# A decoder layer on one core: queries, keys and the MLP's first product computed with tokens on the output's partitions and transposed on TensorE

## The chip, the core and the metric

The kernel runs on one core of one Trainium2 chip. A core has five engines with their own queues: TensorE (PE in the profile; its loads of stationary operands are shown apart as PEld), VectorE (DVE), ScalarE (ACT), GpSimd (POOL) and SyncE (SP), which issues most transfers. The metric is the device time of one execution in microseconds (us). The figure given for a kernel is the median of its runs.

## The reference

One decoder layer for 256 tokens of width 2048. Two mixers with 8 heads each of 128 columns share a normalised input. With 256 tokens and blocks of 256 keys the first mixer is causal attention with ALiBi. The second is causal attention with a cumulated forget gate.

```python
hn = rms_norm(x, norm_mix_g)
z = hn @ w_in
q_a, k_a, v_a, q_b, k_b, v_b, f_logit, g_a, g_b = jnp.split(z, split_idx, axis=-1)
a = moba_attention(split_heads(q_a), split_heads(k_a), split_heads(v_a))
bfx = forgetting_attention(split_heads(q_b), split_heads(k_b), split_heads(v_b), f_logit, b_forget)
merged = jax.nn.sigmoid(g_a) * (merge_heads(a) @ w_proj_a) + jax.nn.sigmoid(g_b) * (merge_heads(bfx) @ w_proj_b)
x = x + merged @ w_out
hm = rms_norm(x, norm_mlp_g)
x = x + jnp.square(jax.nn.relu(hm @ w_up)) @ w_down
return rms_norm(x, norm_final_g)
```

All inputs are float32. `w_in` has 2048 x 10248 elements (four blocks of 1024 columns in it are queries and keys), `w_up` 2048 x 8192, `w_down` 8192 x 2048.

## The kernel before

Every weight is read once, as one stream. `load` brings a chunk of 1 MB (`raw`, 4 buffers) on SP's queue. `emit_split` makes of each half of a chunk a high part `whi` (ACT, line 89) and a low part `wlo` (DVE, line 90), which TensorE takes as float32r; there are 4 buffers of each. The activations are kept in high and low parts too, and a product is the sum of three: high by high, high by low, low by high.

`plan` lists the blocks of the stream in the order of use: values, forget gate and first gate columns, then queries and keys, the other gates, the projections `pa` and `pb`, `w_out`, and the MLP in five groups (`FF_GROUPS`: 16, 16, 16, 8 and 8 tiles of 128 hidden columns), where the `up` blocks of a group stand ahead of its four `down` blocks. A block is worked off half a chunk at a time. After each half `boundary` counts one step, emits the split of a later half, and then emits what tasks are due (`at(step, function)`): attention, head by head in four tasks, transposes of activations, and the like. So the order of the matmuls and of all that stands between them is written out in the program, and each engine runs its queue in that order.

There are two forms of a block:

- `tok_block` (matmul at line 230): the activations of 128 tokens are stationary, 512 columns of weights stream past. The output has tokens on its partitions. One tile of 128 rows of the weights by 512 columns takes 6 matmuls of 512 columns (two halves of the tokens, three products). A half chunk has 2 such tiles, so 12 matmuls.
- `col_block` (lines 243 and 246): 128 columns of weights are stationary, the activations of all 256 tokens stream past, high and low side by side (512 columns, line 243), and then the high ones alone for the low weights (256 columns, line 246). The output has the columns on its partitions, which is what attention and the `down` blocks want as their stationary operands. 128 rows by 512 columns of weights take 4 such pairs. ACT and DVE then add the two halves of the sum (`qk_evac`, `up_evac`).

Queries, keys and `up` are of the second form, everything else of the first. `x_rows` spreads the tokens' scale over the partitions for `qk_evac`. Transposes on TensorE are used for x (line 260), the probabilities (line 412), the merged output (line 483) and x after attention (line 260 again). A result that is read as an operand of `pa`, `pb` or `down` is written to a tile of the pool `head` (tile name `hd`).

Of the kernel before, what the change touches and what calls it, by code (L numbers as in the profile page):

```python
# [7 lines left out]
FT = mybir.dt.float32  # L8
FR = mybir.dt.float32r
AF = mybir.ActivationFunctionType  # L10
OP = mybir.AluOpType
# [4 lines left out]
NT = 2  # L16
# [23 lines left out]
def hybrid_layer(ctx: ExitStack, tc, x, norm_mix_g, w_in, b_forget, w_proj_a, w_proj_b, w_out,  # L40
# [4 lines left out]
    head = ctx.enter_context(tc.tile_pool(name="head", bufs=17))  # L45
# [51 lines left out]
    def seq_tok(src, c0, ncol, nk, k0=0):  # L97
        first = len(halves)
        for k in range(k0, k0 + nk, 4):
            add_chunk(src, k, 4, c0, ncol)  # L100
        return first, len(halves)

    def seq_col(src, c0):
        first = len(halves)
        for k in range(0, KT, 8):
            add_chunk(src, k, 8, c0, 256)
        return first, len(halves)
# [6 lines left out]
    # The 8 forget columns share two blocks of 260 with the first 512 gate columns.  # L114
    plan.append(("fg", 0, seq_tok(w_in, C_F, FG, KT)))
    plan.append(("g", (FG - NH, FG), seq_tok(w_in, C_F + FG, FG, KT)))
    for m in range(2):
        for n in range(NH // 2):
            plan.append(("q", m * NH + 2 * n, seq_col(w_in, (C_QA, C_QB)[m] + n * 256)))
            plan.append(("k", m * NH + 2 * n, seq_col(w_in, (C_KA, C_KB)[m] + n * 256)))  # L120
# [8 lines left out]
    for gi, g in enumerate(FF_GROUPS):  # L129
        for f in range(0, g, 2):  # L130
            plan.append(("up", f0 + f, seq_col(w_up, (f0 + f) * 128)))
        for n in range(4):
            plan.append(("down", (gi, f0, g, n), seq_tok(w_down, n * 512, 512, g, f0)))
        f0 += g
    assert f0 * 128 == DFF

# [65 lines left out]
    def at(n, f, *a):  # L202
        tasks.append((n, f, a))
# [13 lines left out]
    # Tokens on partitions: the activations are stationary, the weights stream.  # L217
# [16 lines left out]
    # Columns on partitions: the weights are stationary, hi and lo activations stream side by side.  # L234
    def col_block(rng, act, ps):
        n = rng[1] - rng[0]
        kh = halves[rng[0]][2]
        for i in range(*rng):
            hi, lo = split[i]
            for kk in range(kh):  # L240
                k = (i - rng[0]) * kh + kk
                for c in range(2):
                    nc.tensor.matmul(ps[c], hi[:, kk, c * 128:(c + 1) * 128],  # L243
                                     act[:, k].rearrange("p s t -> p (s t)"),
                                     start=k == 0, stop=False)
                    nc.tensor.matmul(ps[c][:, S:], lo[:, kk, c * 128:(c + 1) * 128], act[:, k, 0, :],  # L246
                                     start=False, stop=k == n * kh - 1)
            boundary()

# [5 lines left out]
    def transpose_scaled(src, k0, dst, gbase, stepwise=False):  # L255
        """Two column tiles of src (tokens on partitions), transposed, times g, as hi and lo."""
        p = psum.tile([128, 2, S], FT, name="aux")
        for kk in range(2):
            for tok in range(NT):
                nc.tensor.transpose(p[:, kk, tok * 128:(tok + 1) * 128],  # L260
                                    src[:, tok, (k0 + kk) * 128:(k0 + kk + 1) * 128], ident)
        gs = [gcol[:, gbase + k0 + kk:gbase + k0 + kk + 1] for kk in range(2)]

        def high(kk):
            nc.scalar.activation(dst[:, k0 + kk, 0, :], p[:, kk, :], AF.Copy, scale=gs[kk])

# [26 lines left out]
    rk = const.tile([128, S], FT, name="rk")  # L293
    rq = const.tile([128, S], FT, name="rq")
# [15 lines left out]

    def x_rows():
        p = psum.tile([128, 512], FT, name="aux")
        for tok in range(NT):
            nc.tensor.transpose(p[:, tok * 128:(tok + 1) * 128],
                                rstd[:, tok:tok + 1].to_broadcast([128, 128]), ident)
        nc.scalar.activation(rk, p[:, :S], AF.Copy)
        nc.scalar.activation(rq, p[:, :S], AF.Copy, scale=SCALE)
# [4 lines left out]
    at(15, x_rows)  # L322

# [10 lines left out]
    def forget(ps):  # L334
        z = const.tile([128, NT, NH], FT, name="fz")
        e = const.tile([128, NT, NH], FT, name="fe")
        u = const.tile([128, NT, NH], FT, name="fu")
        l = const.tile([128, NT, NH], FT, name="fl")
        for tok in range(NT):
            nc.vector.scalar_tensor_tensor(z[:, tok], ps[tok][:, :NH], rstd[:, tok:tok + 1], bB[:, tok],  # L340
                                           op0=OP.mult, op1=OP.add)
        # log_sigmoid(z) = min(z, 0) - log1p(exp(-|z|)), log1p(e) = log(u) + (e - (u - 1)) / u
        nc.vector.scalar_tensor_tensor(e, z, -1.0, z, op0=OP.mult, op1=OP.min)
        nc.scalar.activation(e, e, AF.Exp)
        nc.vector.tensor_scalar(u, e, 1.0, None, op0=OP.add)
# [25 lines left out]
    def fox_bias(h):  # L371
        p = psum.tile([128, 512], FT, name="aux")
        nc.tensor.matmul(p[:, :S], sel[:, h:h + 1].to_broadcast([64, 128]), cumT, start=True, stop=True)  # L373
        nb = work.tile([128, 384], FT, name="nb")
# [4 lines left out]
    # Scores: columns 0:128 are rows 0:128 on keys 0:128, columns 128:384 rows 128:256 on all keys.  # L379
# [28 lines left out]
    def att_transpose(h):  # L408
# [4 lines left out]
        pt = work.tile([128, 384], FT, name="probT")  # L413
# [3 lines left out]
    def att_values(h):  # L417
# [5 lines left out]
        o = head.tile([128, 2, S], FR, name="hd")  # L423
        nc.scalar.activation(o[:, 0], p[:, :S], AF.Copy)
        nc.vector.tensor_tensor(o[:, 1], p[:, :S], o[:, 0].bitcast(FT), OP.subtract)
        heads[h] = o
# [8 lines left out]

    def qk_evac(kind, h0, ps):
        for c in range(2):
            if kind == "q":
                qk = head.tile([128, 2, S], FT, name="hd")
                heads[h0 + c] = qk  # L440
            qk = heads[h0 + c]
            t = work.tile([128, S], FT, name="ta")
            nc.scalar.activation(t, ps[c][:, :S], AF.Copy)
            nc.vector.tensor_tensor(t, t, ps[c][:, S:], OP.add)
            dst = qk[:, 0 if kind == "q" else 1]
            nc.vector.tensor_tensor(dst, t, rq if kind == "q" else rk, OP.mult)
            state[kind, h0 + c] = dst

# [55 lines left out]
    def up_evac(f, ps):  # L504
        for c in range(2):
            t = work.tile([128, S], FT, name="ta")
            nc.scalar.activation(t, ps[c][:, :S], AF.Copy)  # L507
            nc.vector.tensor_tensor(t, t, ps[c][:, S:], OP.add)  # L508
            u = work.tile([128, S], FT, name="tu")
            nc.vector.scalar_tensor_tensor(u, t, 0.0, t, op0=OP.max, op1=OP.mult)  # L510
            h = head.tile([128, 2, S], FR, name="hd")
            nc.scalar.activation(h[:, 0], u, AF.Copy)  # L512
            nc.vector.tensor_tensor(h[:, 1], u, h[:, 0].bitcast(FT), OP.subtract)  # L513
            hT[f + c] = h
# [14 lines left out]
    def final_add(tok, i):  # L529
        """fst[:, tok, 0] collects the mean square; the first three blocks and EPS come at once."""  # L530
# [22 lines left out]
    for kind, n, rng in plan:  # L553
# [19 lines left out]
        elif kind in ("q", "k"):  # L573
            ps = mm_banks()
            col_block(rng, xT, ps)
            qk_evac(kind, n, ps)
            if kind == "k":
                attention(now[0] + 2, n)
                attention(now[0] + 6, n + 1)
# [7 lines left out]
        elif kind in ("pa", "pb"):  # L587
            m = kind == "pb"
            ps = mm_banks()
            tok_block(rng, lambda k, s, tok: heads[m * NH + k][:, s, tok * 128:(tok + 1) * 128], ps)  # L590
# [16 lines left out]
        elif kind == "up":  # L607
            ps = mm_banks()
            col_block(rng, x1T, ps)
# [7 lines left out]
        else:  # L617
# [4 lines left out]
            def act_h(k, s, tok):  # L622
                return hT[f0 + k][:, s, tok * 128:(tok + 1) * 128]
# [57 lines left out]
```

## Time and profile before

| | |
|---|---|
| time, median of 3 runs | 1386.27 us (1386.09 to 1386.78) |
| span of the profiled execution, first to last instruction | 1385.9 us |
| TensorE busy with matmuls | 1374.7 us, 99% |
| loads of stationary operands (PEld), 6955 of them | 1167.0 us, 84% |
| VectorE busy | 809.8 us, 58% |
| ScalarE busy | 636.6 us, 46% |
| read from HBM | 256.99 MB, 187 GB/s over the span |

The profiled execution's own time is its span, 1385.9 us, and 0.4 us less than the median of the runs. A busy share counts a matmul from its start to a modelled end, and ends overlap the next start. How much of the span a matmul takes is read from the start of one to the start of the next, which is what the chain of work in order of time adds up: each of its pieces has a start, a length and the instructions in it.

### The profile page before, as it was taken

How to read it: one execution, taken by the hardware profiler on the slowest of the kernel's cores; microseconds unless marked ns; L12 is line 12 of the kernel's file. 1: busy time of each engine (PE TensorE's matmuls, PEld its weight loads, DVE VectorE, ACT ScalarE, POOL GpSimd, SP SyncE). 2: the span in 40 equal slices, each digit the busy share in tenths (PEclk: the TensorE clock that was granted, in tenths of full speed). 3: DMA queues.
4: the chain of work that ended last, by engine and by line, in shares of the span. 5: the costliest groups of instructions: out<-in, count | busy, mean ns of one | idle time of the engine just before them, and what ended most of it. 6: DMA issues, size and time to landing. Idle time of an engine off the chain costs nothing.

```text
span 1385.9 us, 17183 instructions
## 1 busy us (share of the span) xinstructions
PE 1374.7 (99%) x6955; PEld 1167.0 (84%) x6955; DVE 809.8 (58%) x1057; ACT 636.6 (46%) x853; POOL 5.8 (0%) x22
## 2 busy tenths in 40 slices
PE   9999999999999999999999999999999999999997
PEld 7889888888888888888888888888888888888886
DVE  6546666666444456655666555665556655566576
ACT  5545544544544443445445434444344443344442
POOL 0000000000000000000000000000000000000000
PEclk9999999999999999999999999999999999999999
DMA  8638555454556565555665655655555565655552
GB/s 307 209 109 258 180 155 175 151 161 153 181 187 199 192 243 194 179 201 180 211 189 183 209 186 182 190 197 191 187 178 183 185 210 195 200 183 186 179 184 90
DMA packets 182223, 260.20 MB, mean 188 GB/s; under 512 B 4576, under 2 KB 109312, under 8 KB 181760
## 3 DMA queue, kind: packets, MB, share of 16 engines
q1 hardware_dynamic: 181424, 255.94, 56.6%
q10 hardware_dynamic: 720, 3.16, 0.6%
q8 instruction: 54, 0.88, 0.3%
q14 instruction: 25, 0.20, 0.0%
HBM read 256.99 MB, written 2.10 MB: 187 GB/s over the span
## 4 chain that ended last, share of the span: by engine, by line
PE 99%; DMA 0%; issue 0%; DVE 0%; SPq 0%; POOLq 0%; POOL 0%; ACT 0%; ACTq 0%
PE mm L230 57%; PE mm L243 26%; PE mm L246 13%; PE aux L384 1%; PE aux L421 0%; PE aux L260 0%; DMA rows<-in_x_dram 0%; PE aux L412 0%; PE aux L422 0%; PE aux L383 0%; PE aux L483 0%; PE aux L373 0%; POOLq L676 0%; POOL fst L540 0%; DVE rows L522 0%
## 5 line engine op out<-in xcount | busy, mean ns | idle before, releaser
L90 DVE TENSOR_TENSOR wlo<-raw,whi 128x1024 fp32r<-128x1024 f32 (+2 forms) x489 | 586.2, 1205 | 470.0 <-ACT whi L89 468.0
L89 ACT ACTIVATE whi<-raw 128x1024 fp32r<-128x1024 f32 (+2 forms) x489 | 505.8, 1042 | 473.0 <-PE mm L230 374.9
L243 PE MATMUL mm<-big,whi 128*128 128x512 f32 x1536 | 547.7, 400 | 0.0
L246 PE MATMUL mm<-big,wlo 128*128 128x256 f32 x1536 | 431.1, 281 | 0.0
L230 PE MATMUL mm<-whi,hd 128*128 128x512 f32 x1280 | 394.4, 388 | 0.0
L243 PEld LDWEIGHTS mm<-big,whi 128*128 128x128 f32 x1536 | 288.4, 188 | 69.0
L230 PE MATMUL mm<-whi,big 128*128 128x512 f32 (+1 forms) x1088 | 326.4, 380 | 0.0
L246 PEld LDWEIGHTS mm<-big,wlo 128*128 128x128 f32 x1536 | 290.2, 189 | 0.6
L230 PEld LDWEIGHTS mm<-whi,hd 128*128 128x128 f32 x1280 | 239.9, 188 | 49.5
L230 PE MATMUL mm<-wlo,hd 128*128 128x512 f32 (+1 forms) x640 | 248.2, 388 | 0.0
L230 PEld LDWEIGHTS mm<-whi,big 128*128 128x128 f32 x1088 | 200.8, 188 | 37.7
L230 PE MATMUL mm<-wlo,big 128*128 128x512 f32 (+1 forms) x544 | 205.5, 378 | 0.0
L230 PEld LDWEIGHTS mm<-wlo,hd 128*128 128x128 f32 x640 | 120.2, 188 | 24.4
L230 PEld LDWEIGHTS mm<-wlo,big 128*128 128x128 f32 x544 | 102.5, 188 | 18.3
L512 ACT ACTIVATE hd<-tu 128x256 fp32r<-128x256 f32 x64 | 26.7, 418 | 62.6 <-DVE tu L510 62.6
L507 ACT ACTIVATE ta<-mm 128x256 f32<-128x256 f32 x64 | 24.1, 376 | 47.3 <-PE mm L246 47.3
L513 DVE TENSOR_TENSOR hd<-tu,hd 128x256 fp32r<-128x256 f32 x64 | 27.2, 425 | 31.0 <-ACT hd L512 31.0
L508 DVE TENSOR_TENSOR ta<-ta,mm 128x256 f32<-128x256 f32 x64 | 26.8, 418 | 20.4 <-ACT ta L507 20.4
L398 ACT ACTIVATE prob<-prob,stat 128x128 f32<-128x128 f32 (+1 forms) x32 | 14.3, 448 | 48.7 <-DVE stat L396 48.7
L510 DVE SCALAR_TENSOR_TENSOR tu<-ta 128x256 f32<-128x256 f32 x64 | 27.2, 425 | 2.2
L518 DVE SCALAR_TENSOR_TENSOR rows<-mm,inv,rows 128x512 f32<-128x512 f32 x32 | 22.5, 744 | 0.0
L414 ACT ACTIVATE probT<-aux 128x384 f32<-128x384 f32 x16 | 7.9, 492 | 30.9 <-PE aux L412 30.9
(117 smaller groups left out, 341.2 us busy)
## 6 DMA issues: line engine op xcount, KB each, us to landing
raw<-in_w_in_dram SPq DMA_DIRECT2D x72, 1024.0 KB, 5.1
raw<-in_w_up_dram SPq DMA_DIRECT2D x64, 1024.0 KB, 5.6
raw<-in_w_down_dram SPq DMA_DIRECT2D x64, 1024.0 KB, 5.2
raw<-in_w_out_dram SPq DMA_DIRECT2D x16, 1024.0 KB, 5.1
raw<-in_w_proj_a_dram SPq DMA_DIRECT2D x8, 1024.0 KB, 5.1
raw<-in_w_proj_b_dram SPq DMA_DIRECT2D x8, 1024.0 KB, 5.0
raw<-in_w_in_dram SPq DMA_DIRECT2D x8, 520.0 KB, 3.8
raw<-in_w_in_dram SPq DMA_DIRECT2D x7, 512.0 KB, 8.0
```

Source lines behind the costliest of these rows:

```text
L89: nc.scalar.activation(hi[:, j:j + n], r[:, j:j + n], AF.Copy)
L90: nc.vector.tensor_tensor(lo[:, j:j + n], r[:, j:j + n], hi[:, j:j + n].bitcast(FT), OP.subtract)
L230: nc.tensor.matmul(p[:, :nc_], a, w[:, kk, c0:c0 + nc_], start=first and j == 0, stop=last and j == 2)
L243: nc.tensor.matmul(ps[c], hi[:, kk, c * 128:(c + 1) * 128], act[:, k].rearrange("p s t -> p (s t)"), start=k == 0, stop=False)
L246: nc.tensor.matmul(ps[c][:, S:], lo[:, kk, c * 128:(c + 1) * 128], act[:, k, 0, :], start=False, stop=k == n * kh - 1)
L398: nc.scalar.activation(t[:, sl], t[:, sl], AF.Exp, bias=st[:, tok:tok + 1], accum_out=st[:, 2 + tok:3 + tok])
L507: nc.scalar.activation(t, ps[c][:, :S], AF.Copy)
L508: nc.vector.tensor_tensor(t, t, ps[c][:, S:], OP.add)
L510: nc.vector.scalar_tensor_tensor(u, t, 0.0, t, op0=OP.max, op1=OP.mult)
L512: nc.scalar.activation(h[:, 0], u, AF.Copy)
L513: nc.vector.tensor_tensor(h[:, 1], u, h[:, 0].bitcast(FT), OP.subtract)
L518: nc.vector.scalar_tensor_tensor(t, ps[tok], inv2[:, tok:tok + 1], t, op0=OP.mult, op1=OP.add)
```

## The change

Queries, keys and `up` use `tok_block` too. Their weights are loaded in blocks of 512 columns. The products then have tokens on the partitions: ACT moves them out of PSUM (scaled by the token's own factor, or through relu and square), and two steps later eight 128 x 128 transposes on TensorE (`transposed_pair`, twice) turn four tiles of columns. For `up` ACT and DVE then make the high and low parts. `col_block` and `x_rows` are gone. The pool of 17 tiles becomes one of 9 tiles of two column tiles each (tile name `pr`). A key block now serves four heads, whose tasks start four steps after it and stand four steps apart, as they did before. Comments are taken out, so that line numbers move: the matmul of `tok_block` is line 230 before and 224 after, the new transposes are line 411, the evacuation of `up` lines 493, 494, 501 and 502.

```diff
-    head = ctx.enter_context(tc.tile_pool(name="head", bufs=17))
+    pair = ctx.enter_context(tc.tile_pool(name="pair", bufs=9))
...
-        for n in range(NH // 2):
-            plan.append(("q", m * NH + 2 * n, seq_col(w_in, (C_QA, C_QB)[m] + n * 256)))
-            plan.append(("k", m * NH + 2 * n, seq_col(w_in, (C_KA, C_KB)[m] + n * 256)))
+        for n in range(NH // 4):
+            plan.append(("q", m * NH + 4 * n, seq_tok(w_in, (C_QA, C_QB)[m] + n * 512, 512, KT)))
+            plan.append(("k", m * NH + 4 * n, seq_tok(w_in, (C_KA, C_KB)[m] + n * 512, 512, KT)))
...
-        for f in range(0, g, 2):
-            plan.append(("up", f0 + f, seq_col(w_up, (f0 + f) * 128)))
+        for f in range(0, g, 4):
+            plan.append(("up", f0 + f, seq_tok(w_up, (f0 + f) * 128, 512, KT)))
...
-    # Columns on partitions: the weights are stationary, hi and lo activations stream side by side.
-    def col_block(rng, act, ps):
...
-                for c in range(2):
-                    nc.tensor.matmul(ps[c], hi[:, kk, c * 128:(c + 1) * 128],
-                                     act[:, k].rearrange("p s t -> p (s t)"),
-                                     start=k == 0, stop=False)
-                    nc.tensor.matmul(ps[c][:, S:], lo[:, kk, c * 128:(c + 1) * 128], act[:, k, 0, :],
-                                     start=False, stop=k == n * kh - 1)
...
+        nc.vector.tensor_scalar(rstq, rstd, SCALE, None, op0=OP.mult)
-
-    def x_rows():
-        p = psum.tile([128, 512], FT, name="aux")
-        for tok in range(NT):
-            nc.tensor.transpose(p[:, tok * 128:(tok + 1) * 128],
-                                rstd[:, tok:tok + 1].to_broadcast([128, 128]), ident)
...
+    def transposed_pair(src, i):
+        p = psum.tile([128, 2, S], FT, name="aux")
+        for c in range(2):
+            for tok in range(NT):
+                nc.tensor.transpose(p[:, c, tok * 128:(tok + 1) * 128],
+                                    src[:, tok, (i + c) * 128:(i + c + 1) * 128], ident)
+        return p
+
     def qk_evac(kind, h0, ps):
+        t = work.tile([128, NT, 512], FT, name="ta")
+        for tok in range(NT):
+            r = rstq if kind == "q" else rstd
+            nc.scalar.activation(t[:, tok], ps[tok], AF.Copy, scale=r[:, tok:tok + 1])
+        for i in range(0, 4, 2):
+            at(now[0] + 2, qk_transpose, kind, h0 + i, t, i)
+
+    def qk_transpose(kind, h, t, i):
+        p = transposed_pair(t, i)
...
+        nc.scalar.activation(qk[:, :, m], p, AF.Copy)
...
     def up_evac(f, ps):
-        for c in range(2):
-            t = work.tile([128, S], FT, name="ta")
-            nc.scalar.activation(t, ps[c][:, :S], AF.Copy)
-            nc.vector.tensor_tensor(t, t, ps[c][:, S:], OP.add)
-            u = work.tile([128, S], FT, name="tu")
-            nc.vector.scalar_tensor_tensor(u, t, 0.0, t, op0=OP.max, op1=OP.mult)
-            h = head.tile([128, 2, S], FR, name="hd")
-            nc.scalar.activation(h[:, 0], u, AF.Copy)
-            nc.vector.tensor_tensor(h[:, 1], u, h[:, 0].bitcast(FT), OP.subtract)
-            hT[f + c] = h
+        t = work.tile([128, NT, 512], FT, name="ta")
+        for tok in range(NT):
+            nc.scalar.activation(t[:, tok], ps[tok], AF.Relu)
+        nc.scalar.activation(t, t, AF.Square)
+        for i in range(0, 4, 2):
+            at(now[0] + 2, up_transpose, f, t, i)
+
+    def up_transpose(f, t, i):
+        p = transposed_pair(t, i)
+        h = pair.tile([128, 2, 2, S], FR, name="pr")
+        nc.scalar.activation(h[:, :, 0], p, AF.Copy)
+        nc.vector.tensor_tensor(h[:, :, 1], p, h[:, :, 0].bitcast(FT), OP.subtract)
+        hT[(f + i) // 2] = h
...
-            col_block(rng, xT, ps)
+            tok_block(rng, act_x, ps)
             qk_evac(kind, n, ps)
             if kind == "k":
-                attention(now[0] + 2, n)
-                attention(now[0] + 6, n + 1)
+                for i in range(4):
+                    attention(now[0] + 4 + 4 * i, n + i)
...
-            col_block(rng, x1T, ps)
+            tok_block(rng, lambda k, s, tok: hl(x1T, k, s, tok), ps)
             up_evac(n, ps)
```

TensorE inside the `up` blocks of the last group, before (`big` is x after attention, transposed; each pair is one `col_block` step):

```order
L243 MATMUL mm<-big,whi 128x512
L246 MATMUL mm<-big,wlo 128x256
L243 MATMUL mm<-big,whi 128x512
L246 MATMUL mm<-big,wlo 128x256
L243 MATMUL mm<-big,whi 128x512
L246 MATMUL mm<-big,wlo 128x256
```

and after (`ta` is the evacuated product of the block before, tokens on partitions):

```order
L224 MATMUL mm<-wlo,big 128x512
L224 MATMUL mm<-whi,big 128x512 x2
L224 MATMUL mm<-wlo,big 128x512
L224 MATMUL mm<-whi,big 128x512
L411 MATMUL aux<-ident,ta 128x128 x8
L224 MATMUL mm<-whi,big 128x512
L224 MATMUL mm<-wlo,big 128x512
L224 MATMUL mm<-whi,big 128x512 x2
```

All matmuls are 512 columns wide now, and once in a block of 96 of them eight transposes stand in between.

TensorE where the first `down` block of the last group begins, before (`hd` is the squared relu, transposed):

```order
L243 MATMUL mm<-big,whi 128x512
L246 MATMUL mm<-big,wlo 128x256
L230 MATMUL mm<-whi,hd 128x512
L230 MATMUL mm<-wlo,hd 128x512
L230 MATMUL mm<-whi,hd 128x512 x2
```

and after, two half chunks into that block, with the numbers of the tiles (`pr_9617` is what is made of the first four transposes, `aux_9612`):

```order
L224 MATMUL mm_9577<-wlo_9551,pr_9467 128x512
L224 MATMUL mm_9577<-whi_9550,pr_9467 128x512
L411 MATMUL aux_9612<-ident_122,ta_9572 128x128 x4
L411 MATMUL aux_9620<-ident_122,ta_9572 128x128 x4
L224 MATMUL mm_9576<-whi_9568,pr_9617 128x512
L224 MATMUL mm_9576<-wlo_9569,pr_9617 128x512
L224 MATMUL mm_9576<-whi_9568,pr_9617 128x512
```

In the two groups of 8 tiles the transposes of the last `up` block stand directly ahead of the matmuls that read their result; in the groups of 16 tiles four half chunks lie between.

ACT over one `up` block, before (two column tiles):

```order
L507 ACTIVATE ta<-mm 128x256
L512 ACTIVATE hd<-tu 128x256
L507 ACTIVATE ta<-mm 128x256
L512 ACTIVATE hd<-tu 128x256
L89 ACTIVATE whi<-raw 128x1024 x4
```

and after (four column tiles):

```order
L493 ACTIVATE ta<-mm 128x512 x2
L494 ACTIVATE ta<-ta 128x1024
L89 ACTIVATE whi<-raw 128x1024 x2
L501 ACTIVATE pr<-aux 128x2x256 x2
L89 ACTIVATE whi<-raw 128x1024 x6
```

The evacuation comes in two parts with two splits of weights between them, where the transposes are waited for.

## Rows read from the trace of the kernel before

**Rows 1.** The page: busy time of TensorE, its granted clock, the chain by engine.
```profile
PE 1374.7 (99%) x6955; PEld 1167.0 (84%) x6955; DVE 809.8 (58%) x1057; ACT 636.6 (46%) x853; POOL 5.8 (0%) x22
...
PEclk9999999999999999999999999999999999999999
...
PE 99%; DMA 0%; issue 0%; DVE 0%; SPq 0%; POOLq 0%; POOL 0%; ACT 0%; ACTq 0%
```

**Rows 2.** Groups by shape on TensorE: names, shapes, count, busy us, mean ns, idle.
```profile
L243 PE MATMUL mm<-big,whi 128*128 128x512 f32 x1536 | 547.7, 400 | 0.0
L246 PE MATMUL mm<-big,wlo 128*128 128x256 f32 x1536 | 431.1, 281 | 0.0
L230 PE MATMUL mm<-whi,hd 128*128 128x512 f32 x1264 | 391.6, 389 | 0.0
...
L230 PEld LDWEIGHTS mm<-whi,hd 128*128 128x128 f32 x1280 | 239.9, 188 | 49.5
```

**Rows 3.** Chain in order of time (start us, length us, what), MLP and output projection.
```profile
514.67 0.87 PE aux L483 x8
...
537.36 0.87 PE aux L483 x8
...
648.94 19.09 PE mm L230 x84
...
757.69 87.08 PE mm L230 x384
935.22 87.06 PE mm L230 x384
1112.72 87.06 PE mm L230 x384
1245.00 43.58 PE mm L230 x192
1333.79 33.73 PE mm L230 x150
```

**Rows 4.** The same chain from the query and key blocks to attention's end.
```profile
119.99 4.28 PE mm L230 x36
...
329.47 2.79 PE mm L230 x12
...
339.89 2.77 PE mm L230 x12
...
353.05 5.50 PE mm L230 x24
358.88 5.47 PE mm L230 x24
365.01 149.66 PE mm L230 x660
```

**Rows 5.** Timeline around one run of eight transposes (start us, busy us, what).
```profile
514.51 1.04 PE L483 MATMUL aux<-ident,big 128*128 128x128 f32 x8
515.14 1.09 ACT L486 ACTIVATE big<-aux 128x512 fp32r<-128x512 f32 x2 [2.10 <-PE aux L483]
515.30 0.47 PE L230 MATMUL mm<-whi,hd 128*128 128x512 f32 x1
515.77 1.29 DVE L487 TENSOR_TENSOR big<-aux,big 128x512 fp32r<-128x512 f32 x2 [1.48 <-ACT big L486]
```

**Rows 6.** Groups by shape on ACT: split of weights, evacuation of 512 columns.
```profile
L89 ACT ACTIVATE whi<-raw 128x1024 fp32r<-128x1024 f32 x471 | 494.7, 1057 | 459.9 <-PE mm L230 362.8 <-PE mm L243 95.0 <-DMA raw<-in_w_in_dram 1.1
L464 ACT ACTIVATE big<-mm,rstd 128x512 f32<-128x512 f32 x14 | 9.5, 688 | 5.7 <-PE mm L230 5.7
```

**Rows 7.** Stretches: busy us of PE, PEld, DVE, ACT, POOL; granted clock; DMA share; GB/s.
```profile
8.50:12.50 4.00, 4.00 (x15) 3.13 (x13) 3.42 (x7) 2.70 (x5) 0.00 (x0) 0.63 1.07 376
514.00:538.00 24.00, 24.00 (x116) 19.99 (x115) 15.08 (x17) 9.64 (x11) 0.00 (x0) 1.00 0.55 188
```

**Rows 8.** Chain in order of time: the first twelve matmuls, and twelve later ones.
```profile
8.73 4.37 PE mm L230 x12
13.53 2.77 PE mm L230 x12
```

More of the change, by code (lines that the diff above doesn't have):

```diff
@@ L101, in seq_tok @@
         return first, len(halves)
[L103 to L107, printed above, removed]
     plan = []
@@ L232, in tok_block @@
             boundary()
-    def col_block(rng, act, ps):
[L236 to L241, printed above, removed]
-                for c in range(2):
-                    nc.tensor.matmul(ps[c], hi[:, kk, c * 128:(c + 1) * 128],
-                                     act[:, k].rearrange("p s t -> p (s t)"),
-                                     start=k == 0, stop=False)
-                    nc.tensor.matmul(ps[c][:, S:], lo[:, kk, c * 128:(c + 1) * 128], act[:, k, 0, :],
-                                     start=False, stop=k == n * kh - 1)
-            boundary()
     def mm_banks():
@@ L292, in hybrid_layer @@
     rstd = const.tile([128, NT], FT, name="rstd")
-    rk = const.tile([128, S], FT, name="rk")
-    rq = const.tile([128, S], FT, name="rq")
+    rstq = const.tile([128, NT], FT, name="rstq")
     def mean_square(acc, dst):
@@ L309, in x_rstd @@
         nc.gpsimd.tensor_tensor(rstd, mean, expo, op=OP.pow)
-    def x_rows():
-        p = psum.tile([128, 512], FT, name="aux")
-        for tok in range(NT):
-            nc.tensor.transpose(p[:, tok * 128:(tok + 1) * 128],
-                                rstd[:, tok:tok + 1].to_broadcast([128, 128]), ident)
-        nc.scalar.activation(rk, p[:, :S], AF.Copy)
-        nc.scalar.activation(rq, p[:, :S], AF.Copy, scale=SCALE)
+        nc.vector.tensor_scalar(rstq, rstd, SCALE, None, op0=OP.mult)
     for j in range(4):
@@ L321, in hybrid_layer @@
     at(11, x_rstd)
-    at(15, x_rows)
     state = {}
@@ L373, in fox_bias @@
         nc.tensor.matmul(p[:, :S], sel[:, h:h + 1].to_broadcast([64, 128]), cumT, start=True, stop=True)
-        nb = work.tile([128, 384], FT, name="nb")
+        nb = work.tile([128, 384], FT, name="nb", bufs=1)
         nc.vector.scalar_tensor_tensor(nb[:, :128], p[:, :128], -1.0, mask[:, :128], op0=OP.mult, op1=OP.add)
@@ L412, in att_transpose @@
             nc.tensor.transpose(p[:, i * 128:(i + 1) * 128], t[:, i * 128:(i + 1) * 128], ident)
-        pt = work.tile([128, 384], FT, name="probT")
+        pt = work.tile([128, 384], FT, name="probT", bufs=1)
         nc.scalar.activation(pt, p[:, :384], AF.Copy)
@@ L422, in att_values @@
         nc.tensor.matmul(p[:, 128:S], v[:, 1, sl], pt[:, S:], start=False, stop=True)
-        o = head.tile([128, 2, S], FR, name="hd")
+        if h % 2 == 0:
+            heads[h // 2] = pair.tile([128, 2, 2, S], FR, name="pr")
+        o = heads[h // 2][:, h % 2]
         nc.scalar.activation(o[:, 0], p[:, :S], AF.Copy)
         nc.vector.tensor_tensor(o[:, 1], p[:, :S], o[:, 0].bitcast(FT), OP.subtract)
-        heads[h] = o
     def attention(n0, h):
@@ L434, in attention @@
         at(n0 + 5, att_values, h)
-    def qk_evac(kind, h0, ps):
-        for c in range(2):
[L438 to L441, printed above, removed]
-            t = work.tile([128, S], FT, name="ta")
-            nc.scalar.activation(t, ps[c][:, :S], AF.Copy)
-            nc.vector.tensor_tensor(t, t, ps[c][:, S:], OP.add)
-            dst = qk[:, 0 if kind == "q" else 1]
-            nc.vector.tensor_tensor(dst, t, rq if kind == "q" else rk, OP.mult)
-            state[kind, h0 + c] = dst
+    def transposed_pair(src, i):
[5 more added lines that the diff above has]
+        return p
+    def qk_evac(kind, h0, ps):
+        t = work.tile([128, NT, 512], FT, name="ta")
[6 more added lines that the diff above has]
+        p = transposed_pair(t, i)
+        if kind == "q":
+            state["qk", h] = pair.tile([128, 2, 2, S], FT, name="pr")
+        qk = state["qk", h]
+        m = 0 if kind == "q" else 1
+        nc.scalar.activation(qk[:, :, m], p, AF.Copy)
+        for c in range(2):
+            state[kind, h + c] = qk[:, c, m]
+        if kind == "k":
+            del state["qk", h]
     gz = merged = x1 = x1T = fin = None
@@ L504, in up_evac @@
     def up_evac(f, ps):
-        for c in range(2):
-            t = work.tile([128, S], FT, name="ta")
-            nc.scalar.activation(t, ps[c][:, :S], AF.Copy)
-            nc.vector.tensor_tensor(t, t, ps[c][:, S:], OP.add)
-            u = work.tile([128, S], FT, name="tu")
-            nc.vector.scalar_tensor_tensor(u, t, 0.0, t, op0=OP.max, op1=OP.mult)
-            h = head.tile([128, 2, S], FR, name="hd")
-            nc.scalar.activation(h[:, 0], u, AF.Copy)
-            nc.vector.tensor_tensor(h[:, 1], u, h[:, 0].bitcast(FT), OP.subtract)
-            hT[f + c] = h
+        t = work.tile([128, NT, 512], FT, name="ta")
[10 more added lines that the diff above has]
+        hT[(f + i) // 2] = h
     def down_evac(n, ps, tok):
@@ L589, in hybrid_layer @@
             ps = mm_banks()
-            tok_block(rng, lambda k, s, tok: heads[m * NH + k][:, s, tok * 128:(tok + 1) * 128], ps)
+            tok_block(rng, lambda k, s, tok: hl(heads[(m * NH + k) // 2], k % 2, s, tok), ps)
             if merged is None:
@@ L622, in act_h @@
             def act_h(k, s, tok):
-                return hT[f0 + k][:, s, tok * 128:(tok + 1) * 128]
+                return hl(hT[(f0 + k) // 2], k % 2, s, tok)
             if not last:
```

## The prediction

> **What bounds the kernel now.** I read the page first. TensorE is busy 99% of the span, the chain that ended last lies on it for 99%, and the clock granted to it is full in all 40 slices [rows 1]. No other engine is near: DVE 58%, ACT 46%. So the time is the sum of TensorE's queue, instruction after instruction, and the question is what each costs there. The mean durations do not say it: a 512-wide matmul of the column form "takes" 400 ns and its 256-wide partner 281 ns, a 512-wide one of the token form 389 ns [rows 2], but 1536 pairs at 681 ns would be 1046 us, three quarters of the span, for work that the chain holds for about 540. These ends are modelled and overlap. I therefore read the chain in order of time, where a piece runs from the start of its first instruction to the start of the next piece [rows 3, 4]. The reader is to see there that nothing waits: the pieces follow each other without holes through the MLP.
>
> **The price of a matmul, token form.** A group of four `down` blocks is 384 matmuls and 87.06 us [rows 3], so 226.7 ns each. The 192 of a small group take 43.58 us [rows 3], 227.0 ns.
>
> **The price of the column form.** Between two `down` groups lie the `up` blocks. From 757.69 + 87.08 to 935.22 are 90.45 us; from 935.22 + 87.06 to 1112.72 are 90.44; from 1112.72 + 87.06 to 1245.00 are 45.22; from 1245.00 + 43.58 to 1333.79 are 45.21; and from 648.94 + 19.09 to 757.69 are 89.66, with one run of eight transposes of x in it [rows 3]. Together 360.98 us. A large group has 256 pairs, so 353 ns a pair. Per 128 columns of weights both forms stream 768 columns; the column form does it in 2 matmuls (353 ns), the token form in 1.5 (340 ns). The change wins 13 ns per pair.
>
> **The price of the transposes.** Two runs of eight (line 483) start at 514.67 and 537.36, 22.69 us apart, with the 96 matmuls of one block between them [rows 3]. 96 at 226.7 ns are 21.76, so a run costs 0.93 us, including the slower matmuls just behind it. The chain gives 0.87 for the run alone [rows 3]. I take 0.93; the new runs are the same instruction, size and place, between two token-form matmuls. The change adds 24 runs: 16 behind the `up` blocks, 8 behind the query and key blocks.
>
> **MLP.** After: 1536 matmuls, four times 87.06 or 348.2 us, and 17 runs (16 new, the one of x), 15.8 us: 364.0. Before: 361.0. Plus 3.0 us.
>
> **Queries, keys and attention.** From 119.99 + 4.28 to 365.01 are 240.74 us [rows 4]. In them lie 512 pairs, 132 matmuls of the gates (the nine chain pieces from 329.47 to 358.88, counts added [rows 4]), and all tasks of 16 heads. After, the pairs are 768 matmuls; with the 132 they are 900, or 204.0 us. The tasks of the heads are the same instructions, now all between token-form matmuls; their price there is to be read at the end of the stretch. From 339.89 to 353.05 are 13.16 us with 48 matmuls (10.88) and one full set of a FoX head's tasks: 2.28 us. From 353.05 to 358.88 are 24 matmuls and one transpose of probabilities, 0.39; from 358.88 to 365.01 24 matmuls and one product with the values, 0.69 [rows 4]. A MoBA head has scores (priced as the values), transpose and values: 1.77. Eight of each are 32.4 us. With 8 runs of transposes (7.4) the sum is 243.8. Plus 3.1 us. `x_rows` goes with two transposes, a quarter of a run: minus 0.2.
>
> **A new wait.** The queue order shows that in the two groups of 8 tiles the last transposes stand directly ahead of the matmuls that read what ACT and DVE make of them. The nearest rows are those of line 483, the same shapes [rows 5]: from the run's start, ACT begins its first copy at 0.63 us and needs half of 1.09, so the high part is there at 1.2; DVE begins at 1.26 and needs half of 1.29, so the low part is there at 1.9. TensorE would go on at 0.79. It waits until 1.2 and then loads the operand, 188 ns [rows 2]: about 0.6 us; the third matmul wants the low part at 1.85 and gets it at 1.9 plus the load, about 0.3 more. 0.9 us in each of two places, 1.8 in all. Bounds: nothing, if the copy is earlier than in those rows, and 2 us a place, if one split of 1.06 us [rows 6] happens to stand ahead of the copy. A gain is excluded, since nothing waits there now. In the three groups of 16 four half chunks (10.9 us) lie between, which covers the 1.9.
>
> **Costed at nothing.** The evacuations: behind each block ACT has two moves of 0.69 us, a square of 1.06 (priced as a split of the same size [rows 6]) and perhaps a split of 1.06, 3.5 us, and the transposes come two half chunks, 5.4 us, behind the block's end. If that cover went, TensorE would wait in 24 places. DVE loses three operations for each column tile and gains one wide one for two; it was not on the path. The weights' loads keep their bytes; of ACT's idle time ahead of the splits the data accounts for 1.1 us in all [rows 6].
>
> **Sum.** 3.0 + 3.1 - 0.2 + 1.8 = 7.7 us on the profiled 1385.9, which lies 0.4 us under the median; so 1386.3 + 7.7, and the predicted time is 1394.0 us, 0.55% slower. The two effects nearly cancel: 2304 matmuls in place of 1536 pairs win about 18 us, 24 runs of transposes cost 22, the waits and the dearer neighbourhood of the heads' tasks are the rest.
>
> **Rivals.** (1) *A shorter interval of the token form in its new place; not slower.* For it: the column form has two speeds in the same program, 88.8 us for the first `up` group (89.66 less 0.87) and 90.45 for the second [rows 3], so an interval is not fixed by shape alone. Against it: every long token stretch shown lies at 226.7 to 227.0 ns [rows 3], with different activations. 2.1 ns less on each of 2304 matmuls (4.9 us) would bring the time within 0.2% of before, 3.3 ns to 1386; below 222 ns the change would be faster by more than that. 0.10: 0.06 for no difference, about 1387, 0.04 for faster, about 1383.
>
> (2) *The clock falls at the transposes.* At the start of the program TensorE ran at a granted share of 0.63 on average, that is partly at 1.2 GHz and partly at 2.4, after it had stood idle for data [rows 7]; there 12 matmuls took 4.37 us where later 2.77 [rows 8], 1.6 us more. If each of the 24 runs did the same, 38 us: 1432. The trace speaks against it: with line 483's runs in the stretch the clock is 1.00 [rows 7]. The Trainium skill ("TensorE: Matmul & The Clock Gate", Part 4: PE-mode transpose) says that a transpose takes some 275 ns in a kernel and does not count as activity that brings the full clock. By its 275 ns the 192 transposes would cost 53 us, an estimate, in place of 22; the trace differs, 0.87 us for eight, 109 ns from start to start, at full clock. 0.02.
>
> (3) *The transposes wait for ACT behind every block.* The cover is 5.4 us against 3.5; attention's exponentials share ACT beside the query and key blocks. It decides from 2 us of delay on; each microsecond beyond that costs 24 us if it holds everywhere and 8 us at queries and keys alone: 1400 to 1418. Against it: half of ACT's time is idle. 0.08.
>
> **How the numbers follow.** The forecast has 0.80. Its own range: without the new waits and with 0.87 us a run it is 1394.0 - 1.8 - 1.4, or 1390.8; with 2 us a place, 1396.2, and some tenths for what the heads' tasks cost in another order. I give 1390.5 to 1397.5, which leaves the rivals out. A measurement of this kernel tells about 0.2% (2.8 us) from no change: faster 0.04, same 0.06, slower 0.90.
>
> **What would show it.** Right: the clock at full share; each `up` group of 16 tiles at 90.7 us from chain to chain (87.06 and four runs); runs of line 411 at 0.87 us; a hole of about 1 us ahead of the line 224 matmuls two half chunks into the first `down` block of groups four and five, ended by ACT and then by DVE, and none in the first three groups. Wrong: an `up` stretch whose matmuls are not 227 ns apart, a wait of line 411 for ACT, or a granted share below 1 after the first 20 us.

## The result, and the profile after

The changed kernel takes 1394.37 us (median of 4 runs, 1394.32 to 1394.42). The kernel before takes 1386.53 us beside it. The ratio is 1.0051, with a 95% interval of 1.004 to 1.0063. The change makes the layer half a percent slower; 1394.0 was predicted. The span of the profiled execution grew by 6.8 us, from 1385.9 to 1392.7.

The page of the changed kernel, in the lines that answer to [rows 1]: busy time, granted clock in 40 slices, and the last chain by engine.

```profile
PE 1380.3 (99%) x6377; PEld 1147.4 (82%) x6377; DVE 729.3 (52%) x834; ACT 652.4 (47%) x803; POOL 5.8 (0%) x22
...
PEclk9999999999999999999999999999999999999999
...
PE 98%; ACT 1%; DMA 0%; DVE 0%; issue 0%; SPq 0%; POOLq 0%; POOL 0%; ACTq 0%
```

TensorE has 578 matmuls fewer (of 6955) and its chain is longer. The granted clock shows the highest digit in all slices as before, and it is 1.00 on average from 20 to 1380 us. (The digit 9 stands for 90% or more, so it does not say that the clock was full throughout: between 8.5 and 12.5 us the granted share was 0.62 here and 0.63 before [rows 7].) VectorE lost 80 us of work, for which TensorE had not waited. New is 1% of ACT in the chain: somewhere TensorE waits for it. The chain counts the whole work on which a wait hangs, so that share is larger than the wait.

The chain of the changed kernel in order of time (start us, length us, what), which answers to [rows 3, 4]:

```profile
119.42 31.50 PE mm L224 x156
...
518.55 21.80 PE mm L224 x96
...
629.18 21.80 PE mm L224 x96
...
699.90 21.80 PE mm L224 x96
722.58 21.78 PE mm L224 x96
745.23 21.80 PE mm L224 x96
767.90 108.84 PE mm L224 x480
...
1376.16 4.12 PE mm L224 x18
```

Three places in the chain of the kernel before that the third reading below needs, beside [rows 3, 4]:

```profile
515.54 21.81 PE mm L230 x96
...
626.26 21.81 PE mm L230 x96
...
1369.29 4.12 PE mm L230 x18
```

Three readings. First, 480 matmuls in 108.84 us are 226.75 ns each, over most of four `down` blocks, the next group's first `up` block and the start of its second: the token form costs in its new place what it cost in its old ones. Second, two blocks of `up` start 22.68, 22.65 and 22.67 us apart; 96 matmuls are 21.76, so a run of eight transposes costs 0.91 us. Third, the lengths of two stretches between places that both kernels have. From the start of the query blocks' piece (119.99 before, 119.42 after) to the first block behind the merged output's first transposes (515.54 before, 518.55 after) there are 395.55 us before and 399.13 after, 3.58 more. From the last full `w_out` piece (626.26 before, 629.18 after) to the last 18 matmuls (1369.29 before, 1376.16 after) there are 743.03 and 746.98, 3.95 more. Below, these are **stretch A** and **stretch B**. Their sum is 7.5. Ahead of them the changed kernel is 0.6 us shorter: 0.3 is data that came earlier at the start, and 0.2 the two transposes of `x_rows`.

What TensorE waited for in the changed kernel (engine line, waited for, us in total, times, longest):

```profile
PE aux L238 <- DMA rows<-in_x_dram: 2.1, 1, 2.1
PE aux L141 <- DVE junk L135: 1.1, 1, 1.1
PE aux L381 <- DVE prob L375: 0.6, 1, 0.6
PE mm L224 <- ACT pr L501: 0.5, 2, 0.2
```

The first two are the start of the program, and the kernel before has them too. The last is the wait that was forecast, in two places. The third was not.

**The forecast wait.** Timeline of TensorE in the first of the two places, two half chunks into the first `down` block of the fourth group (start us, busy us, what, idle before it):

```profile
1254.66 1.03 PE L411 MATMUL aux<-ident,ta 128*128 128x128 f32 x8
1255.94 0.50 PE L224 MATMUL mm<-whi,pr 128*128 128x512 f32 x1 [0.25 <-ACT pr L501]
1256.28 0.40 PE L224 MATMUL mm<-wlo,pr 128*128 128x512 f32 x1
1256.67 0.50 PE L224 MATMUL mm<-whi,pr 128*128 128x512 f32 x1
```

The first matmul starts 1.28 us after the start of the run, where [rows 5] had 0.79, and the third, which reads the low part from DVE, starts 0.39 us after the second in place of 0.23. By the starts of the matmuls ten further on, the place costs 0.79 us more than a run without a reader behind it, and the other one 0.80.

**The wait that was not forecast.** The chain near the end of attention, in the changed kernel:

```profile
380.94 1.28 ACT L454
...
383.20 1.04 ACT big L454
...
385.29 1.06 ACT whi L89
...
386.37 1.22 DVE wlo L90
```

and its end in the timeline:

```profile
387.85 0.15 DVE L373 RECIPROCAL stat<-stat 128x2 f32<-128x2 f32 x1
388.04 0.55 DVE L375 TENSOR_SCALAR prob<-prob,stat 128x128 f32<-128x128 f32 x2
388.38 0.70 PE L381 MATMUL aux<-ident,prob 128*128 128x128 f32 x3 [0.56 <-DVE prob L375]
```

Line 454 is the sigmoid of the first gate columns, a table load and two operations of 1.05 us. Behind it on ACT stand the gates' own evacuation and a split. The split's low part holds DVE's queue, and the last step of the last head's softmax (lines 373 and 375) stands behind it on DVE. TensorE stands at that head's transposes. By the starts of the matmuls around it, that run of three costs 1.29 us, where the other fifteen of its kind cost 0.36 to 0.40: a stall of 0.9 us. In the kernel before, the same table load is here:

```profile
365.04 0.39 ACT L424 ACTIVATE hd<-aux 128x256 fp32r<-128x256 f32 x1 [2.31 <-PE aux L422]
...
377.06 1.28 ACT L468 ACT_TABLE_LOAD   x1
```

The last head was done (line 424 writes its result) 12 us ahead of it. A key block now serves four heads, which start 4, 8, 12 and 16 steps behind it. Before, it served two, which started 2 and 6 steps behind it: the spacing of four steps stayed, the first start did not. So the last head is 10 steps later behind its key block, and attention ends 30 us later, in the sigmoid.

### The profile page after: what moved, and what is told of

The parts are those of the page before. It is cut to its first block, busy times and chain, and to the rows that moved or that the text cites. A ratio compares the mean times of both kernels' runs of the same rounds, so it can differ in the third digit from the quotient of the medians.

```text
span 1392.7 us, 15770 instructions
## 1 busy us (share of the span) xinstructions
PE 1380.3 (99%) x6377; PEld 1147.4 (82%) x6377; DVE 729.3 (52%) x834; ACT 652.4 (47%) x803; POOL 5.8 (0%) x22
## 4 chain that ended last, share of the span: by engine, by line
PE 98%; ACT 1%; DMA 0%; DVE 0%; issue 0%; SPq 0%; POOLq 0%; POOL 0%; ACTq 0%
PE mm L224 93%; PE aux L411 1%; PE aux L353 1%; PE aux L238 0%; PE aux L390 0%; PE aux L381 0%; DMA rows<-in_x_dram 0%; PE aux L352 0%; PE aux L469 0%; PE aux L391 0%; PE aux L342 0%; ACT L454 0%; DVE wlo L90 0%; ACT pr L501 0%; ACT big L454 0%
## 5 line engine op out<-in xcount | busy, mean ns | idle before, releaser
L224 PE MATMUL mm<-whi,big 128*128 128x512 f32 (+1 forms) x2624 | 818.3, 389 | 0.0
L224 PEld LDWEIGHTS mm<-whi,big 128*128 128x128 f32 x2624 | 489.2, 188 | 97.1
L224 PE MATMUL mm<-wlo,big 128*128 128x512 f32 (+1 forms) x1312 | 504.4, 384 | 0.0
L224 PE MATMUL mm<-whi,pr 128*128 128x512 f32 x1280 | 395.6, 389 | 0.5 <-ACT pr L501 0.5
L224 PEld LDWEIGHTS mm<-wlo,big 128*128 128x128 f32 x1312 | 247.0, 188 | 47.0
L224 PEld LDWEIGHTS mm<-whi,pr 128*128 128x128 f32 x1280 | 239.8, 188 | 50.7 <-ACT pr L501 1.0
L224 PE MATMUL mm<-wlo,pr 128*128 128x512 f32 (+1 forms) x640 | 248.2, 388 | 0.0
L224 PEld LDWEIGHTS mm<-wlo,pr 128*128 128x128 f32 x640 | 120.2, 188 | 24.6
L411 PE MATMUL aux<-ident,ta 128*128 128x128 f32 x192 | 24.9, 273 | 0.0
L411 PEld LDWEIGHTS aux<-ident,ta 128*128 128x128 f32 x192 | 22.3, 140 | 3.1
```

What stands on the lines that cost most here:

```text
L224: nc.tensor.matmul(p[:, :nc_], a, w[:, kk, c0:c0 + nc_], start=first and j == 0, stop=last and j == 2)
L411: nc.tensor.transpose(p[:, c, tok * 128:(tok + 1) * 128], src[:, tok, (i + c) * 128:(i + c + 1) * 128], ident)
```

## The experiments

All times are read as stretches A and B of the profiled execution, from the same pieces of the chain as above, since medians of whole runs scatter by about 1 us. Both stretches repeat to 0.1 us wherever a kernel leaves them alone.

| kernel | time, us (before beside it) | stretch A | stretch B |
|---|---|---|---|
| before | | 395.55 | 743.03 |
| changed | 1394.37 (1386.53) | 399.13 | 746.98 |
| up_alone | 1391.88 (1387.62) | 395.55 | 747.03 |
| qk_alone | 1391.22 (1387.62) | 399.13 | 742.97 |
| up_one_step | 1393.42 (1387.08) | 399.12 | 745.37 |
| late_sigmoid | 1393.00 (1387.08) | 398.19 | 746.98 |
| no_waits | 1392.08 (1387.38) | 398.20 | 745.40 |
| runs_twice | 1414.66 (1387.08) | 406.10 | 760.07 |

### One part of the change alone

In `up_alone` queries and keys keep the column form, with the code of the kernel before for their blocks, evacuation and `x_rows`. In `qk_alone` the `up` blocks do. The tile `ta` has one buffer in both, to make room. Of the first edit, the lines that choose the form:

```diff
-            tok_block(rng, act_x, ps)
+            col_block(rng, xT, ps)
             qk_evac(kind, n, ps)
```

> Only up in the token form with transposes; queries and keys in the column form as before. My theory, by the parts of the changed kernel's trace: 2.6 us for matmuls and transposes, less 0.3 for the matmuls behind a change of form, and 1.6 for the two waits: 3.9 us over the kernel before, 1390.4 us. Rival: the cost lies at the queries and keys and their attention; then within 1 us of before.

> Only queries and keys in the token form with transposes; up in the column form as before. My theory: 2.7 us for matmuls, transposes and the tasks of the heads between them, 0.9 for the wait beside the sigmoid, less 0.3 for the two transposes of the scale that went: 3.4 us over the kernel before, 1389.9 us. Rival: the cost lies in the MLP; then within 1 us of before.

Stretch B carries the whole cost of the one (4.0 us) and stretch A that of the other (3.58). The parts add up to the whole change and neither rival holds: 1.0029 (interval 1.0018 to 1.0041) and 1.0023 (1.0014 to 1.0033) times before.

### The transposes behind `up` one step earlier

```diff
-            at(now[0] + 2, up_transpose, f, t, i)
+            at(now[0] + 1, up_transpose, f, t, i)
```

> The changed kernel, with the transposes behind an up block one step after it instead of two. My theory: the two waits behind the last up block of the small groups (0.79 and 0.80 us in the changed kernel's trace) go, since a half chunk (2.7 us) then lies between the transposes and the matmuls that read them, and ACT's square is done 0.8 us before the transposes start; about 1.6 us less than the changed kernel, 1392.8 us. Rival: the transposes now wait for ACT's square behind all 16 up blocks; some tenths each, 1394 us or more.

The same place in the chain of this kernel:

```profile
1253.10 0.87 PE aux L411 x8
1253.97 65.32 PE mm L224 x288
```

The run is followed by its matmuls without a hole. Stretch B is 1.61 us shorter, the 1.6 of the two waits, and no wait of line 411 for ACT appears. One step is cover enough.

### The sigmoid one block later

```diff
-            if c0 == 1024:
+            if c0 == 1536:
                 g_late(c0)
-            g_evac(c0, ncol, ps, AF.Copy if c0 < 1024 else AF.Sigmoid)
+            g_evac(c0, ncol, ps, AF.Copy if c0 < 1536 else AF.Sigmoid)
```

> The changed kernel, with the sigmoid of the first gate columns (its table load and two operations on ACT) one gate block later, when attention is over. My theory: the wait of the last head's transposes (0.9 us, behind a DVE queue that waits for ACT) goes and nothing takes its place; 0.9 us less than the changed kernel, 1393.5 us. Rival: the wait is the head's own chain of work at the end and not ACT's sigmoid; then it stays and the time is 1394.4 us.

The sigmoid then covers 1536 columns in its two operations, in place of 1024, and starts 20 us later. Stretch A is 0.94 us shorter, and TensorE's list of waits has lost line 381:

```profile
PE aux L238 <- DMA rows<-in_x_dram: 2.4, 1, 2.4
...
PE mm L224 <- ACT pr L501: 0.5, 2, 0.2
```

So the wait was ACT's sigmoid and not the head's own chain.

### Both waits away

> The changed kernel with both moves at once: the transposes behind an up block after one step, and the first sigmoid one gate block later. Theory: the three waits were all that TensorE waited for, so the two savings add up (1.60 us in the MLP, 0.93 us beside attention): 2.5 us less than the changed kernel in span, and what is left over the kernel before, some 5 us, is matmuls and transposes alone. Rival: one of the waits comes back elsewhere, and less than 2 us go.

The edit is the two above together. A and B are 0.93 and 1.58 us shorter; the savings add up and nothing comes back. All that TensorE waits for in this kernel:

```profile
PE aux L238 <- DMA rows<-in_x_dram: 2.1, 1, 2.1
PE aux L141 <- DVE junk L135: 1.1, 1, 1.1
```

Both stand at the start of the program. The kernel is still 1.0037 times before (1.0023 to 1.0051): 2.65 us in A and 2.37 in B are matmuls and transposes alone.

### Every new transpose twice

```diff
-            for tok in range(NT):
+            for tok in 2 * tuple(range(NT)):
                 nc.tensor.transpose(p[:, c, tok * 128:(tok + 1) * 128],
                                     src[:, tok, (i + c) * 128:(i + c + 1) * 128], ident)
```

> The changed kernel, with each of the 192 new transposes issued twice into the same place. My theory: a transpose costs what it takes from start to start, 0.109 us, wherever it stands, so 192 more are 20.9 us: 1415.3 us, at the same granted clock. Rival one: the cost of a run lies in switching between matmuls and transposes and not in their number; then a few us, 1397 or less. Rival two: longer runs of transposes let the clock fall; then the granted share drops below 0.99 and the time lies above 1430 us.

```profile
704.74 1.75 PE aux L411 x16
706.49 21.78 PE mm L224 x96
```

A run of sixteen takes 1.75 us where one of eight takes 0.87 or 0.88, so 0.109 us for each, and the 96 matmuls behind it keep their time. A grows by 6.97 us (64 transposes at 0.109), B by 13.09 (128 would be 13.95; the rest is the two waits, which a longer run covers in part: each costs 0.36 us here, where it cost 0.8). The granted clock of the whole execution is 0.998, and 0.997 without them. So the cost goes with the number of transposes. Switching to them and back costs the 0.04 us by which a run's 0.91 exceeds its 0.87, and the clock does not fall.

### The two spacings of the column form

Rival (1) rested on the two speeds of the column form [rows 3]: its pairs were 353.3 ns apart in four groups of `up` blocks and 346.7 in the first, which alone has a run of transposes one step in. Is it the run? The kernel before was given one in each of the others:

```diff
+    def extra_run():
+        p = psum.tile([128, 512], FT, name="aux")
+        for i in range(8):
+            nc.tensor.transpose(p[:, i % 4 * 128:(i % 4 + 1) * 128], ident, ident)
...
+            if n in (16, 32, 48, 56):
+                at(now[0] + 1, extra_run)
             col_block(rng, x1T, ps)
```

> The kernel before, with a run of eight transposes of a constant (results unused) one step into the second to fifth group of up blocks, where the first group has its eight transposes of x. In the trace of before, the pairs of the column form are 346.7 ns apart behind such a run in the first group and 353.3 ns in the other groups. Theory: the run sets the faster spacing; 768 pairs times 6.6 ns win 5.1 us, four runs cost 3.5, so about 1.6 us less than before, 1384.9 us, and the other up groups take 89.7 us and 44.9 us in place of 90.45 and 45.2. Rival: the spacing has another cause, and the runs only cost: 1390.0 us.

The `down` groups of this kernel, between which the `up` groups lie:

```profile
758.00 87.08 PE mm L230 x384
934.75 87.08 PE mm L230 x384
1111.50 87.08 PE mm L230 x384
1243.87 43.56 PE mm L230 x192
1332.72 33.71 PE mm L230 x150
```

The `up` groups take 89.67, 89.67, 45.29 and 45.29 us with a run of 0.87 in each, so 88.80 and 44.42 without it, against 90.45, 90.44, 45.22 and 45.21 [rows 3]. The pairs behind the run are 346.7 ns apart in all four. The kernel is 0.9994 times before (0.9985 to 1.0003), since the runs eat most of the gain. Shorter runs should keep the faster spacing at a lower cost. One kernel had one, two, four and six transposes in the four groups:

> The kernel before, with one transpose of a constant one step into the second group of up blocks, two in the third, four in the fourth and six in the fifth, where the run before had eight in each. Theory one: any interruption by a transpose sets the faster spacing of the column form; then all four groups have pairs 346.7 ns apart, and one transpose (about 0.1 us) buys 1.7 us in a large group. Theory two: it is the place in time at which the pairs start again, so that some lengths set it and others leave 353.3 ns; the runs of three in attention leave it nearly always. Theory three: it takes all eight; then 353.3 ns in all four. Time of the whole, by theory one, about 1383 us.

All four groups had 346.7 ns; 1383.86 us beside 1386.18, one run of each. The `down` groups around the third `up` group, which had two transposes:

```profile
933.48 87.07 PE mm L230 x384
1109.55 87.07 PE mm L230 x384
```

That group takes 89.00 us. So one should do everywhere:

> The kernel before, with one transpose of a constant (result unused) one step into each of the second to fifth group of up blocks. Theory: the faster spacing of the column form, set by a single transpose as in the run with one, two, four and six of them; the MLP takes 704.9 to 705.2 us in place of 709.6, and the kernel lies 4.5 us (0.3%) under the kernel before. Rival: in the small groups one transpose is not enough; then 1.5 us less of that.

It came out 0.9976 times before (0.9968 to 0.9985), 1383.83 us beside 1387.38, which with the kernel above is the fastest of this study. But the rival held:

```profile
758.61 87.08 PE mm L230 x384
934.59 87.07 PE mm L230 x384
1110.56 87.08 PE mm L230 x384
1242.16 43.55 PE mm L230 x192
1331.03 33.70 PE mm L230 x150
```

The `up` groups take 88.90, 88.90, 44.52 and 45.32: the fifth stayed at 353.4 ns a pair. Two in each should mend that:

> The kernel before, with two transposes of a constant in each of the second to fifth group of up blocks. With one in each, the fifth group kept pairs 353.4 ns apart, and the others had 346.7. Theory: two set the faster spacing in all four, as they did in the third group of the run with one, two, four and six; the MLP takes 705.1 us (709.6 less 5.1, plus four times 0.16), 0.7 us less than with one. Rival: which group keeps the slower spacing is not a matter of the number of transposes; then again one group or another stays at 353.3 ns.

```profile
758.41 87.08 PE mm L230 x384
936.15 87.10 PE mm L230 x384
1113.90 87.10 PE mm L230 x384
1246.43 43.53 PE mm L230 x192
1335.39 33.68 PE mm L230 x150
```

It did the opposite: 90.66, 90.65, 45.43 and 45.43, the slower spacing everywhere plus the two transposes, and 1.0006 times before (0.9997 to 1.0015). My theory that any interruption sets the spacing has fallen, and so has the one that the number decides: two set the faster spacing in the third group of one kernel and not in that of another. What decides it stays open. Shown is that the column form has two steady spacings with the same instructions, that a restart can move it from the slower to the faster one, and that eight transposes did so in all five groups of before_extra_run.

The kernel before also has the faster spacing where no transpose stands among the pairs. The first and the 80th matmul of line 243 in the query blocks:

```profile
124.10 0.39 PE L243 MATMUL mm<-big,whi 128*128 128x512 f32 x1
...
151.50 0.39 PE L243 MATMUL mm<-big,whi 128*128 128x512 f32 x1
```

The 79 distances between them are 27.40 us, 346.8 ns each, and the first task of attention stands behind them. Ahead of them stand token-form matmuls of 260 columns, and ahead of the slow groups such of 512. Behind that task the distances that hold no task are 353 ns, but for a dozen of 346.7. So a run of transposes is one way to the faster spacing and not a condition of it.

## Why the prediction was right

**The sum, term by term.**

| term | predicted, us | found, us | from |
|---|---|---|---|
| MLP, matmuls and transposes | +3.0 | +2.4 | stretch B of no_waits |
| the two waits in the small groups | +1.8 | +1.6 | up_one_step |
| queries, keys, attention's tasks | +3.1 | +2.65 | stretch A of no_waits |
| `x_rows` | -0.2 | -0.2 | ahead of stretch A |
| the sigmoid in attention's end | not seen | +0.9 | late_sigmoid |
| sum | +7.7 | +7.3 | |

The span grew by 6.8: data came 0.3 us earlier, and the pieces between and behind the stretches are 0.1 us shorter each.

**The base of the sum** was off, and that the total of 1394.0 lies so near 1394.37 is in part luck. The forecast put its 7.7 us on the median of three runs and took the profiled execution, with its span of 1385.9 us, to be 0.4 us faster than that median. But the time given for an execution is longer than its span, by 1.7 us in most: the changed kernel's profiled execution has 1394.42 and 1392.7, and an execution of the kernel before with that span of 1385.9 has 1387.59. Spans differ by 6.8 us and the medians side by side by 7.8. Against the four medians of 15 runs of the kernel before that stand beside the experiments (1387.08 to 1387.62) the changed kernel is 6.8 to 7.3 us slower. So the forecast of the difference was 0.4 to 0.9 us too high by these, and 0.1 too low by the first medians.

**The price of a matmul** held to the digit: 226.7 ns forecast, 226.75 found. That it was taken from starts and not from durations was the step on which all else hung: by the mean durations of [rows 2] the token form would have won 100 ns per pair of the column form, some 150 us in all.

**The price of a run** was 0.93 forecast, 0.91 found. The two hundredths over 17 runs are 0.3 us. Another 0.24 are the slower first matmuls behind a change of form, which went with the column form: in the kernel before the first ten or so of a `down` group start 224 to 241 ns apart, 0.04 to 0.06 us more in a group than at 226.7. Together they are the 0.6 us by which the MLP's term was too large.

**The new wait** was found where it was put, in the two small groups and nowhere else, ended by ACT and then by DVE: 0.79 and 0.80 us in place of 0.9. The rows of line 483 were the right ones: ACT and DVE take in the new place what they took there.

**Attention's tasks** were priced between token-form matmuls at 32.4 us. Of the 0.45 us by which this term was too large, 0.16 are the eight runs at 0.91; what the rest is, no run shows. What failed there is a step that was not taken: the tasks were treated as the same instructions in another neighbourhood, with "some tenths" for their order. The move of each last head by 10 steps was in the queue order for all to see, and what stands on ACT at the steps to which they move was not looked up. It was the sigmoid with its table load, 0.93 us. The terms' sum came within half a microsecond (7.7 for 7.3) because the MLP's and the attention's terms were 1 us too large together; two errors cancelled.

**Rival (1)**, a shorter interval of the token form, did not occur: all long stretches lie at 226.7. Its reason, that an interval is not fixed by shape, is true of the column form, as the last four experiments show, and it speaks for the kernel before and not for the change: of the 18 us that the change wins on matmuls, 5 are there only because the four later groups of `up` blocks ran at the slower of the two spacings (6.6 ns on 768 pairs), and by an estimate 2 more because most pairs of the query and key blocks did (6.6 ns on the 334 distances of some 353 ns).

**Rival (2)**, the clock, was excluded twice: the granted share is 1.00 from 20 us to the end of the matmuls after the change, and also with twice the transposes. The Trainium skill's rule ("TensorE: Matmul & The Clock Gate", Part 4: PE-mode transpose) that transposes do not count as activity has no effect here, with 1.75 us of them at a stretch at most and 2.7 us of matmuls or more between; whether it holds for longer stretches no run here shows. **Rival (3)**, a wait behind every block, did not occur, even with one step of cover.

The weight loads are a caution of the same kind as the durations. The share of the span with a load under way fell from 84% to 82% while the time rose. There are fewer loads (6377 for 6955), and those of the transposes are shorter (140 ns against 188 on the profile's page). The Trainium skill ("Perfetto Trace Analysis", Identifying the Most-Contended Engine) names the loads' summed durations over the span, beside the share of peak arithmetic, as measures of how near TensorE is to its limit, in place of the matmuls' busy share. That sum fell further here, from 1304.7 us (94%) to 1185.1 us (85%). The chain's starts told the time; none of these shares did.

## What to carry to other kernels

Where TensorE is busy from end to end, price both layouts of a product by the distance from start to start in the kernel's own chain, and add what turns the result: here 2304 wide matmuls for 1536 pairs won 18 us and 24 runs of eight transposes cost 22. When tasks move along a queue, look up what the other engines do at the steps to which they move, one-time work like a table load above all. A run of transposes whose result is read at once makes TensorE wait for ACT and DVE (0.8 us a place here); one step more between them hid that.

## What the runs showed of the hardware

- The same pairs of matmuls (512 and 256 columns) repeat every 346.7 ns or every 353.3 ns for a whole group of blocks; an interruption by a single transpose switched from the slower to the faster in some groups and not in another, and what decides it is not known. The token form's matmuls of 512 columns showed one spacing, 226.7 ns, apart from the first ten or so behind an interruption.
- A 128 x 128 float32 transpose costs 109 ns from start to start in runs of eight and of sixteen, while its duration in the groups is 273 ns.
